# Post-normed products with tokens in the rows, and four tiles of the next products side by side

## The chip, the cores and the metric

The kernel runs on one core of a Trainium2 chip. The metric is the device time of one execution in microseconds. TensorE (PE) multiplies matrices into PSUM, which has eight banks of 512 fp32 columns; VectorE (DVE), ScalarE (ACT) and GpSimd (POOL) work on rows of 128 partitions; SyncE (SP) issues the loads. [...]

## What is computed

A block with a post-normed mixer and a post-normed feed-forward, followed by two layers of a second block, for 256 tokens of 1024 features. The change touches the first block and the start of the second:

```python
y = concatenate([out_a, out_b, out_c], axis=-1) @ w_out[l]
x = x + rmsnorm(y, norm_post_mix[l])
h = rmsnorm(x, norm_pre_ffn[l])
f = square(relu(h @ w_ff1[l])) @ w_ff2[l]
x = x + rmsnorm(f, norm_post_ffn[l])
# second block, layer 0, begins with
x = x + 0.5 * swiglu(rmsnorm_2(x, ffn_norm1[0]), ffn1_wg[0], ffn1_wu[0], ffn1_wd[0])
```

## The kernel before

The residual is kept as `x[k]`, eight tiles of 128 features by 256 tokens (features in the partitions). Every product is made of three matmuls on parts rounded to fp32r: `xh` (rounded) and `xl` (what is left) of the data, `wh` and `wl` of the weights: wh*xh, wh*xl, wl*xh (`mm_t`, lines 134 to 141; `mm_n`, 143 to 151, has the tokens as the stationary operand and 128 tokens in the rows of the result). A pre-norm is not applied to x: its gain goes into xh and xl, and its factor per token into the result.

Weights come through the class `Stream` (72 to 129) in one fixed order. `dma` loads a chunk of up to 2048 columns on SyncE into one of three buffers; `split` casts a part of 1024 columns on ScalarE (line 102); `low` subtracts on VectorE (line 112) and, after a chunk's last part, issues the next load; there are six slots (`HL`) for split parts. `get(ahead)` first splits until `ahead` more parts than the one asked for are there (4 by default), then returns the part. `low` of a part is written out when the next part is split, or in `get` when at most two parts are in hand. `fill` splits up to six parts with the subtraction on GpSimd.

The order of the instructions on each engine is the order in which the program writes them (`manual_schedule`, line 154), so a wait holds up all that is written later for the same engine. The tile pools add the semaphores; a new PSUM tile waits for a bank that is no longer read.

**The mixer's end** (791 to 818). The gating matmuls (line 796) make mixed tiles 0 to 2. `out_proj` (451) makes eight feature tiles of y, 24 matmuls of 256 columns each; `y_evac` (478) squares each in ScalarE and adds the squares up on GpSimd (`add_sq`, 193), and copies y times its gain. Then four blocks of 24 short matmuls for the position bias (`t5_mm`, 512) lie between the column sums (`colsum`, line 219), mean (226), power -0.5 on GpSimd (188), the diagonal matrix `dg` (234), and a matmul that broadcasts the factors to all rows (239). `post_add` (526) multiplies y by it, adds it to x on VectorE or GpSimd, and makes xh on ScalarE and xl on VectorE, tile by tile.

**The feed-forward** (828 to 894). The first two tiles of h @ w_ff1 are made side by side, k by k, as xh and xl arrive (841 to 845); then 15 pairs of tiles follow (852), each with its evacuation `ev_ff` (834), the squares of x for the pre-norm, and the bias blocks' evacuation `t5_evac` (521). The second product makes eight feature tiles of 96 matmuls each and ends like the mixer.

**`ffn2`** (383 to 434) is the second block's feed-forward. At its first call `start` (920) makes the squares of x; the gate and the up tile of the first pair are made one after the other for k = 0 to 6, then both for k = 7; then follow the second pair, with the column sums between its halves, the broadcast, two evacuations, and the loop over 20 more pairs.

## Time and profile before

| | |
|---|---|
| median of 3 runs | 1280.71 us (1280.48 to 1282.17) |
| profiled execution | 1278.97 us, its span 1277.1 us |
| TensorE, matmuls | busy 1250.2 us, 98% of the span |
| VectorE | busy 846.4 us, 66% |
| ScalarE | busy 661.3 us, 52% |
| GpSimd | busy 197.3 us, 15% |
| granted TensorE clock, mean | 0.989 of full |
| loads | 208.71 MB, 164 GB/s over the span |

Times are microseconds from the span's start. Busy time of TensorE includes the tail of each matmul, which overlaps the next, so the distance between two starts tells the rate. "PEld" is the load of the stationary operand. In a row of the waits, the engine and line ahead of the arrow stood idle until the one behind it was done. `L139` is line 139 of the kernel. A group by line and form gives the count, the busy time, the mean of one in ns, and the idle time ahead of them. [...]

### The profile page before, as it was taken

What the parts mean: (1) busy time and instruction counts of PE and PEld (TensorE: products, weight loads), DVE (VectorE), ACT (ScalarE), POOL (GpSimd) and SP (SyncE); (2) the same over time, 40 slices, a digit from 0 to 9 for tenths busy, and PEclk for the clock granted to TensorE, in tenths of its full rate; (3) what the DMA queues carried; (4) which work ended last, traced back from release to release, by engine and by line L of the source; (5) the groups of instructions that cost most, each with busy time, mean ns of one, the idle gap of its engine ahead of it and who ended that gap; (6) DMA issues with size and microseconds to landing.
All of it is one profiled execution on the core that took longest, in us unless ns stands there. A gap on an engine that the chain in (4) does not pass through costs nothing.

```text
span 1277.1 us, 24835 instructions
## 1 busy us (share of the span) xinstructions
PE 1250.2 (98%) x10316; PEld 1202.9 (94%) x10316; DVE 846.4 (66%) x1490; ACT 661.3 (52%) x1174; POOL 197.3 (15%) x192
## 2 busy tenths in 40 slices
PE   8999899999899999999999999999999989999998
PEld 7879899999799999977999999999999868999998
DVE  6886676654587666676766666666666796666553
ACT  5557465444345444565654444545454787554442
POOL 4424210110420001210300001100001462100000
PEclk9999899999899999999999999999999999999999
DMA  7534355555135545530455546556556411555463
GB/s 233 194 105 160 104 195 196 200 208 188 67 132 199 199 139 192 208 123 34 165 198 199 177 157 205 191 178 217 168 163 204 165 66 67 181 186 195 157 199 107
DMA packets 37265, 211.37 MB, mean 166 GB/s; under 512 B 4768, under 2 KB 8224, under 8 KB 18848
## 3 DMA queue, kind: packets, MB, share of 16 engines
q1 hardware_dynamic: 37152, 209.78, 48.3%
q8 instruction: 81, 1.33, 0.4%
q14 instruction: 32, 0.26, 0.1%
HBM read 208.71 MB, written 1.05 MB: 164 GB/s over the span
## 4 chain that ended last, share of the span: by engine, by line
PE 88%; DVE 6%; issue 2%; ACT 2%; DMA 1%; POOL 0%; SPq 0%; ACTq 0%; POOLq 0%; DVEq 0%
PE ps L139 26%; PE ps L140 26%; PE ps L141 26%; DVE wl L112 2%; PE ps L297 2%; PE ps L323 2%; PE ps L308 1%; PE ps L149 1%; PE ps L150 1%; PE ps L151 1%; PE ps L325 1%; ACT wh L102 1%; DVE dg L234 0%; PE ps L219 0%; DVE kc L1169 0%
## 5 line engine op out<-in xcount | busy, mean ns | idle before, releaser
L139 PE MATMUL ps<-xh,wh 128*128 128x256 f32 (+1 forms) x1848 | 523.0, 283 | 1.6 <-ACT xh L531 1.6
L140 PE MATMUL ps<-xl,wh 128*128 128x256 f32 (+1 forms) x1848 | 520.3, 282 | 1.5 <-DVE xl L538 0.8
L141 PE MATMUL ps<-xh,wl 128*128 128x256 f32 (+1 forms) x1848 | 518.9, 281 | 2.4 <-DVE wl L112 2.4
L112 DVE TENSOR_TENSOR wl<-raw,wh 128x1024 fp32r<-128x1024 f32 (+3 forms) x434 | 489.2, 1166 | 46.4 <-ACT wh L102 45.4
L102 ACT CAST wh<-raw 128x1024 fp32r<-128x1024 f32 (+4 forms) x436 | 400.2, 959 | 62.5 <-PE ps L140 26.5
L139 PEld LDWEIGHTS ps<-xh,wh 128*128 128x128 f32 (+1 forms) x1848 | 350.3, 190 | 5.3 <-issue 3.2
L140 PEld LDWEIGHTS ps<-xl,wh 128*128 128x128 f32 (+1 forms) x1848 | 349.8, 189 | 3.4 <-DVE xl L538 2.0
L141 PEld LDWEIGHTS ps<-xh,wl 128*128 128x128 f32 (+1 forms) x1848 | 350.0, 189 | 2.7 <-DVE wl L112 2.6
L139 PE MATMUL ps<-ah,wh 128*128 128x256 f32 x960 | 267.8, 279 | 0.0
L140 PE MATMUL ps<-al,wh 128*128 128x256 f32 x960 | 267.8, 279 | 0.0
L141 PE MATMUL ps<-ah,wl 128*128 128x256 f32 x960 | 267.8, 279 | 0.0
L139 PEld LDWEIGHTS ps<-ah,wh 128*128 128x128 f32 x960 | 180.4, 188 | 0.0
L140 PEld LDWEIGHTS ps<-al,wh 128*128 128x128 f32 x960 | 180.4, 188 | 0.0
L141 PEld LDWEIGHTS ps<-ah,wl 128*128 128x128 f32 x960 | 180.4, 188 | 0.0
L199 POOL TENSOR_TENSOR acc<-acc,sq 128x256 f32<-128x256 f32 x42 | 49.9, 1188 | 587.0 <-ACT sq L198 586.9
L393 ACT ACTIVATE s<-t 128x256 f32<-128x256 f32 x88 | 36.8, 418 | 191.9 <-DVE t L391 191.9
L391 DVE TENSOR_TENSOR t<-ps,rb 128x256 f32<-128x256 f32 x88 | 37.2, 423 | 73.5 <-PE ps L141 68.2
L213 DVE TENSOR_TENSOR al<-f,ah 128x256 fp32r<-128x256 f32 (+1 forms) x105 | 48.9, 466 | 52.8 <-ACT ah L212 52.8
L212 ACT CAST ah<-f 128x256 fp32r<-128x256 f32 (+1 forms) x105 | 45.9, 437 | 55.8 <-DVE f L395 43.2
L252 ACT ACTIVATE xh<-x,cols 128x256 fp32r<-128x256 f32 x40 | 20.4, 510 | 102.6 <-DVE x L428 95.6
L395 DVE TENSOR_TENSOR f<-ps,s 128x256 f32<-128x256 f32 x88 | 37.3, 424 | 47.4 <-ACT s L393 47.4
L427 DVE SCALAR_TENSOR_TENSOR t<-ps,rb 128x256 f32<-128x256 f32 x32 | 13.6, 425 | 76.2 <-PE ps L141 76.2
(285 smaller groups left out, 1321.4 us busy)
## 6 DMA issues: line engine op xcount, KB each, us to landing
raw<-in_gu SPq DMA_DIRECT2D x88, 1024.0 KB, 4.9
raw<-in_dn SPq DMA_DIRECT2D x64, 704.0 KB, 4.3
raw<-in_ff SPq DMA_DIRECT2D x32, 1024.0 KB, 5.0
raw<-in_w_out SPq DMA_DIRECT2D x4, 1024.0 KB, 4.9
raw<-in_aq SPq DMA_DIRECT2D x4, 1024.0 KB, 5.1
raw<-in_a_out SPq DMA_DIRECT2D x4, 1024.0 KB, 5.0
raw<-in_b_out SPq DMA_DIRECT2D x4, 1024.0 KB, 4.8
raw<-in_w1q SPq DMA_DIRECT2D x6, 512.0 KB, 4.0
```

The costliest lines, as they stand in the source:

```text
L102: act.copy(h[:, :n], t)
L112: eng.tensor_tensor(out=lo, in0=t, in1=h.bitcast(F32), op=ALU.subtract)
L139: pe.matmul(ps, lhsT=h[:, c:c + m], rhs=x[0][k], start=s0, stop=False)
L140: pe.matmul(ps, lhsT=h[:, c:c + m], rhs=x[1][k], start=False, stop=False)
L141: pe.matmul(ps, lhsT=lo[:, c:c + m], rhs=x[0][k], start=False, stop=s1)
L199: gp.tensor_tensor(out=acc, in0=acc, in1=sq, op=ALU.add)
L212: act.copy(h, src)
L213: dve.tensor_tensor(out=lo, in0=src, in1=h.bitcast(F32), op=ALU.subtract)
L297: pe.matmul(ps[:, o:o + n], lhsT=u["q"][:, i * P:i * P + P], rhs=u["k"][:, :n], start=True, stop=True)
L391: dve.tensor_tensor(out=t, in0=g, in1=rb, op=ALU.mult)
L393: act.activation(out=s, in_=t, func=AF.Silu)
L395: dve.tensor_tensor(out=f, in0=u, in1=s, op=ALU.mult)
```

## The change

- `w_out` and `w_ff2` are packed so that a part holds 512 columns of w for two rows-tiles (feed-forward), or 1024 columns for one (mixer). `mm_y` makes their products with 128 tokens of the data as the stationary operand and 512 features moving: four PSUM banks `py[tt][h]` hold y with tokens in the rows.
- In the mixer the k-tiles run in the order 3 to 7, 0 to 2; the gating matmuls stand behind the third of them; the last two run bank by bank.
- A Square with a running sum on ScalarE (`y_sq`) replaces the squares, their sums on GpSimd and the column sums. `y_rstd` makes the factors. `y_scale` copies y out of PSUM times the factor of its row, ScalarE for the first 128 tokens and VectorE for the others. There is no diagonal and no broadcast.
- `PostAdd.turn` transposes one feature tile of y with two TensorE transposes; VectorE multiplies by the gain and adds x; `prep` (250) makes xh, the square of x and its sum, and xl of the tile before.
- `PostAdd.products` makes four tiles of the next products side by side in two banks: two turns ahead of each k from 1 to 3, and one split at k = 4. Ahead of it stand the fourth bias block and four `get` calls, which leave five (4, 3, 2, 1 ahead) parts in hand.
- `ffn2` takes these as its first two pairs (`begun`), makes the third pair with the column sums between, and builds `dg` on ScalarE. The bias blocks are evacuated one pair later in the feed-forward, and in `ffn2` from its fourth pair on.
- `fill`, `post_add`, `y_evac`, `start` and the squares of x inside the loops are gone.

The diff, cut to its core:

```diff
-        def fill(self):
-            while self.ns < self.ng + HL and self.split(gp):
-                pass
...
+    def mm_y(banks, w, n, x, kts, first, last):
+        for tt in range(2):
+            for j in range(len(banks[tt])):
+                h, lo = w
+                ts = slice(tt * P, tt * P + P)
+                for i, k in enumerate(kts):
+                    c = (i * len(banks[tt]) + j) * n
...
+                    pe.matmul(ps, lhsT=x[0][k][:, ts], rhs=h[:, c:c + n], start=s0, stop=False)
+                    pe.matmul(ps, lhsT=x[1][k][:, ts], rhs=h[:, c:c + n], start=False, stop=False)
+                    pe.matmul(ps, lhsT=x[0][k][:, ts], rhs=lo[:, c:c + n], start=False, stop=s1)
...
+            if begun:
+                p = bank()
+                mm_t(p[:, :T], ws.get(), 0, P, X, range(KT), True, True)
+                _, rs = norm_cols(acc)
+                dg = tp.tile([P, T], F32, tag="dg", bufs=1, name="dg")
+                for tt in range(2):
+                    act.activation(out=dg[:, tt * P:tt * P + P], in_=ident, func=AF.Copy, scale=rs[:, tt:tt + 1])
+                mm_t(p[:, T:], ws.get(), 0, P, X, range(KT), True, True)
+                rb = bcast(rs, dg=dg)
+                for j, p in enumerate(begun + [p]):
+                    evac(j, p[:, :T], p[:, T:], rb)
...
+    def y_sq(ps, ss, tt, h, junk):
+        act.activation(out=junk, in_=ps, func=AF.Square, accum_out=ss[:, h, tt:tt + 1])
...
+        ms = sm.tile([P, 2], F32, tag="ms", bufs=3, name="ms")
+        dve.scalar_tensor_tensor(out=ms, in0=ss[:, 1], scalar=1.0 / D, in1=s0, op0=ALU.mult, op1=ALU.add)
+        rs = sm.tile([P, 2], F32, tag="rs", bufs=3, name="rs")
+        rstd_pow(rs, ms, 2)
...
+    def y_scale(ps, y, rs, pieces):
+        for h, o, n in pieces:
...
+            act.activation(out=dst[0], in_=src[0], func=AF.Copy, scale=rs[:, 0:1])
+            dve.tensor_scalar(out=dst[1], in0=src[1], scalar1=rs[:, 1:2], scalar2=None, op0=ALU.mult)
...
+        def turn(self):
...
+            ps = bank()
+            for tt in range(2):
+                pe.transpose(ps[:, tt * P:tt * P + P], self.y[tt][:, d * P:d * P + P], ident)
+            dve.scalar_tensor_tensor(out=x[d], in0=ps[:, :T], scalar=gcol(self.gi, d), in1=x[d], op0=ALU.mult, op1=ALU.add)
+            prep(d, self.gnext, self.acc)
+            if d == KT - 1:
+                prep_end()
+        def products(self, outs, w):
+            for k in range(KT):
+                if k:
+                    self.turn()
+                    self.turn()
+                for i, (p, wi) in enumerate(zip(outs, w)):
+                    mm_t(p, wi, 0, P, X, [k], k == 0 and i % 2 == 0, k == KT - 1 and i % 2 == 1)
+                if k == 4:
+                    ws.split()
+                    ws.low()
...
+        w = [ws.get(), ws.get(3)]
+        ws.low()
+        for tt in range(2):
+            for h in range(2):
+                for i in range(2):
+                    mm_y([[py[tt][h]] if t == tt else [] for t in range(2)], [v[:, 512 * h:512 * h + 512] for v in w[i]], 512,
+                         (oh, ol), [MIX_ORDER[KT - 2 + i]], False, i == 1)
+                y_sq(py[tt][h], ss, tt, h, pp.tile([P, 512], F32, tag="s", bufs=2, name="junk"))
+        t5 = [t5_mm([o5[:, i]]) for i in range(3)]
+        rs_y = y_rstd(ss, None)
+        y_scale(py, y, rs_y, ((0, 0, T), (0, T, T)))
+        acc = new_acc()
+        add = PostAdd(y, 1, 2, acc)
+        add.turn()
+        add.turn()
+        y_scale(py, y, rs_y, ((1, 0, 2 * T),))
         t5.append(t5_mm([o5[:, 3]]))
-        acc = post_add(ys, rb, 2)
+        w = [ws.get(HL - 2 - i) for i in range(4)]
+        p = [bank() for _ in range(2)]
+        add.products([b[:, o:o + T] for b in p for o in (0, T)], w)
```

The feed-forward's end has the same lines as the mixer's, behind `mm_y` over two halves of 16 parts, with `ws.get()` for each part and `ws.low()` after it in the second half.

## Rows read from the trace of the kernel before

**Rows 1.** TensorE's waits, whole run: who waited <- for whom: us, times, longest.
```profile
PE ps L239 <- DVE dg L234: 6.1, 3, 2.7
```

**Rows 2.** Windows at boundary 1: us, busy (count) by engine, granted clock, DMA share, GB/s.
```profile
131.00:139.50 8.50, 5.13 (x109) 4.45 (x107) 5.43 (x11) 3.64 (x6) 3.35 (x3) 0.95 0.43 153
139.50:145.50 6.00, 5.95 (x28) 5.95 (x29) 5.42 (x12) 3.05 (x6) 4.96 (x6) 0.51 0.01 3
```

**Rows 3.** Timeline at boundary 1: start, us, engine, operation, [idle before <- releaser].
```profile
130.99 0.87 PE L517 MATMUL ps<-rbd,o 128*128 128x64 bf16 x24
...
132.77 0.16 DVE L226 TENSOR_SCALAR ms<-ps 128x2 f32<-128x2 f32 x1 [1.38 <-PE ps L219]
...
133.00 0.71 POOL L188 TENSOR_TENSOR rs<-ms,mhalf 128x2 f32<-128x2 f32 x1 [3.21 <-DVE ms L226]
...
133.69 2.34 POOL L112 TENSOR_TENSOR wl<-raw,wh 128x1024 fp32r<-128x1024 f32 x1
...
133.75 2.56 DVE L234 TENSOR_SCALAR dg<-kon,rs 128x128 f32<-128x128 f32 x2 [0.82 <-POOL rs L188]
...
136.36 0.70 PE L239 MATMUL ps<-dg,kon 128*128 128x256 f32 x2 [2.21 <-DVE dg L234]
...
138.57 0.58 PE L139 MATMUL ps<-xh,wh 128*128 128x256 f32 x1 [0.81 <-ACT xh L531]
...
153.39 0.28 PE L139 MATMUL ps<-xh,wh 128*128 128x256 f32 x1
...
158.99 0.28 PE L139 MATMUL ps<-xh,wh 128*128 128x256 f32 x1
```

**Rows 4.** Windows at boundary 2, same columns as group 2.
```profile
321.80:329.50 7.70, 4.61 (x108) 4.18 (x106) 4.15 (x8) 2.80 (x5) 3.03 (x2) 1.00 0.14 55
329.50:336.50 7.00, 6.21 (x21) 4.98 (x22) 6.38 (x16) 4.09 (x9) 5.26 (x6) 0.52 0.00 0
336.50:340.00 3.50, 3.50 (x18) 3.50 (x18) 3.29 (x6) 2.25 (x8) 2.35 (x3) 0.50 0.02 5
```

**Rows 5.** Timeline of TensorE at boundary 2.
```profile
321.85 0.87 PE L517 MATMUL ps<-rbd,o 128*128 128x64 bf16 x24
...
349.23 0.70 PE L239 MATMUL ps<-dg,kon 128*128 128x256 f32 x2 [1.18 <-DVE dg L234]
...
355.37 0.28 PE L139 MATMUL ps<-xh,wh 128*128 128x256 f32 x1
```

**Rows 6.** Timeline of TensorE, products of 512 columns in latent attention; ten intervals.
```profile
1001.48 0.40 PE L150 MATMUL ps<-wh,cl 128*128 128x512 f32 x1
...
1003.80 0.40 PE L151 MATMUL ps<-wl,ch 128*128 128x512 f32 x1
```

**Rows 7.** Timeline of TensorE, four transposes in attention and what follows.
```profile
97.17 0.60 PE L308 MATMUL ps<-kon,p 128*128 128x128 f32 x4
...
97.70 0.65 PE L323 MATMUL ps<-pt,vm 128*64 128x256 f32 x2
```

**Rows 8.** Groups by line and form: count | busy us, mean ns | idle before.
```profile
L486 ACT ACTIVATE y<-ps,cols 128x256 f32<-128x256 f32 x16 | 7.7, 482 | 0.0
...
L836 ACT ACTIVATE t<-ps 128x512 f32<-128x512 f32 x15 | 9.0, 599 | 23.4 <-PE ps L141 23.4
...
L271 ACT ACTIVATION_READ_ACCUMULATOR p<-s,nm 128x1 f32 x44 | 8.3, 190 | 0.0
...
L427 DVE SCALAR_TENSOR_TENSOR t<-ps,rb 128x256 f32<-128x256 f32 x32 | 13.6, 425 | 76.2 <-PE ps L141 76.2
...
L252 ACT ACTIVATE xh<-x,cols 128x256 fp32r<-128x256 f32 x40 | 20.4, 510 | 102.6 <-DVE x L428 95.6 <-DVE x L470 6.8
...
L261 DVE SCALAR_TENSOR_TENSOR xl<-x,cols,xh 128x256 fp32r<-128x256 f32 x44 | 22.6, 514 | 15.4 <-ACT xh L252 14.2 <-ACT xh L531 1.2
...
L102 ACT CAST wh<-raw 128x1024 fp32r<-128x1024 f32 x293 | 295.7, 1047 | 30.4 <-PE ps L140 15.1 <-DMA raw<-in_w1q 6.4 <-DMA raw<-in_w1k 2.7
...
L112 DVE TENSOR_TENSOR wl<-raw,wh 128x1024 fp32r<-128x1024 f32 x291 | 360.9, 1273 | 39.0 <-ACT wh L102 38.5
```

More of the change, by code (lines that the diff above doesn't have):

```diff
@@ L380, in warm_table, with ffn2 @@
         act.activation(out=t, in_=mhalf[:, 0:1], func=func)
-    def ffn2(acc, gnext, extra=(), start=None, more=()):
+    def ffn2(acc, gnext, extra=(), begun=None):
         extra = list(extra)
@@ L597, in block_kernel @@
         mem = [mem_[:, k] for k in range(KT)]
-        mh = [mp.tile([P, T], F32R, tag=f"mh{k}", name=f"mh{k}") for k in range(KT)]
+        mh_ = mp.tile([P, KT, T], F32R, tag="mh", name="mh")
+        mh = [mh_[:, k] for k in range(KT)]
         ml_ = mp.tile([P, KT, T], F32R, tag="ml", name="ml")
@@ new lines, in block_kernel @@
+        while not pipe.done():
+            pipe.step()
+        y_ = mp.tile([P, 2, D], F32, tag="mh", name="y")
+        y = [y_[:, tt] for tt in range(2)]
+        ss = sm.tile([P, 2, 2], F32, tag="ss", name="ss")
+        py = [[bank() for _ in range(2)] for _ in range(2)]
+        for i, k in enumerate(MIX_ORDER):
+            if i == 3:
+                gmlp_out()
+                warm_table(AF.Silu)
+            if i < KT - 2:
+                mm_y(py, ws.get(), 512, (oh, ol), [k], i == 0, False)
@@ new lines, in block_kernel @@
+        w = [ws.get(), ws.get(3)]
+        ws.low()
+        for tt in range(2):
+            for h in range(2):
[4 more added lines that the diff above has]
+        t5 = [t5_mm([o5[:, i]]) for i in range(3)]
@@ L889, in block_kernel @@
-        dve.tensor_tensor(out=fy, in0=fy, in1=r2, op=ALU.mult)
-        dg = diag(fy)
-        ws.fill()
-        rb = bcast_ps(dg)[:, :T]
+        ss = sm.tile([P, 2, 2], F32, tag="ss", name="ss")
+        eps = sm.tile([P, 2], F32, tag="eps", name="eps")
+        dve.scalar_tensor_tensor(out=eps, in0=ms_f, scalar=EPS, in1=ms_f, op0=ALU.mult, op1=ALU.mult)
+        py = [[bank() for _ in range(2)] for _ in range(2)]
+        for h in range(2):
+            for i in range(16):
+                if h == 0 and i % 4 == 0:
+                    t5_mask(4 + i // 4, n5, o5[i // 4])
+                mm_y([[py[tt][h]] for tt in range(2)], ws.get(), 512, (AH, AL), [2 * i, 2 * i + 1], i == 0, i == 15)
+            if h:
+                ws.low()
+            for tt in range(2):
+                y_sq(py[tt][h], ss, tt, h, ft.tile([P, 2 * T], F32, tag="tf"[tt], name="junk"))
@@ L893, in block_kernel @@
+        t5 = [t5_mm(o5[i]) for i in range(3)]
+        rs_y = y_rstd(ss, eps)
+        y_scale(py, y, rs_y, ((0, 0, T), (0, T, T)))
+        acc = new_acc()
+        add = PostAdd(y, 3, g2("ffn_norm1_2", 0), acc)
+        add.turn()
+        add.turn()
+        y_scale(py, y, rs_y, ((1, 0, 2 * T),))
         t5.append(t5_mm(o5[3]))
-        acc = post_add(ys, rb, g2("ffn_norm1_2", 0))
+        w = [ws.get(HL - 2 - i) for i in range(4)]
+        p = [bank() for _ in range(2)]
+        add.products([b[:, o:o + T] for b in p for o in (0, T)], w)
@@ L916, in t5_step @@
                 return f
[L918 to L930 removed]
+            acc = ffn2(acc, g2("mix_norm_2", 0), [t5_step(j) for j in range(4, 16)], p)
         if upto == 3:
```

180 lines of the change are left out of this document (63 added, 117 removed), and 2 rows, old and new, of the table seq.

## The prediction

> **What bounds the kernel now.** TensorE is busy for 98% of the span, so a gain can come only from its pauses, its clock, or fewer cycles. The list of TensorE's waits is short, and its longest entry is the broadcast that waits for the diagonal `dg` [rows 1]. That sends the reader to the two places where a post-normed product meets the residual: the end of the mixer's output product (boundary 1, from 131 us) and the end of the first feed-forward (boundary 2, from 322 us). The windows show more there than the waits do: at boundary 1, 28 products take 6.0 us at a granted clock of 0.51 [rows 2]; at boundary 2, 21 products take 7.0 us and 18 more 3.5 us, all at about half clock [rows 4]. At full clock a product of 256 columns follows the one before it after 0.1167 us: 48 of them lie between 153.39 and 158.99 [rows 3]. I count from S, the end of the stream of products before each boundary (130.99 [rows 3], 321.85 [rows 5]), to the start of the 145th product behind it, so that both kernels have done the same work.
>
> Before, boundary 1: 158.99 - 130.99 = 28.0 us [rows 3]; 144 products alone are 16.8. The chain is to be seen in the same rows: the last Square, the sums, the power at 133.00, then the two diagonals, which take 2.56 us because GpSimd's split (2.34 us) runs beside them; the first product comes at 138.57, 7.6 us after S. Boundary 2: 355.37 - 321.85 = 33.5 us [rows 5]. It is dearer because one gate tile first consumes xh and xl as they arrive, three products at a time, and because a second broadcast waits 1.2 us [rows 5].
>
> **The change, part by part.** *Wider products.* 192 products of 256 columns become 96 of 512 in the mixer, 768 become 384 in the feed-forward. At full clock ten intervals of 512 columns take 2.32 us [rows 6], 0.232 each against 2 x 0.1167 = 0.2334: 480 x 0.0014 = 0.6 us saved (bounds 0 and 1.0). *Moved gating matmuls, moved sums of squares, changed weight order, later bias evacuations*: 0, since the stages where they lie are unbroken products, which cover them (the list of waits has nothing long there [rows 1]); without that cover an evacuation more, under 1 us. The residual's squares now sit in the chain and are counted there on ScalarE and GpSimd. Removed: 8+8 accumulations, the column sums at S, both diagonals and broadcasts, and GpSimd's splits.
>
> *The new chain*, the same at both boundaries. Square with a running sum over 512 columns: no row shows it; the Relu of 512 from PSUM is 0.60 and the read of a sum 0.19 [rows 8], so I take 0.86 between 0.6 and 1.1. From S: the last product's tail is 0.40 - 0.23 [rows 6], so Square starts at 0.2 and ends at 1.1; mean 0.16, power 0.71 [rows 3], 2.05; scaled copies of 256 columns on ScalarE, like those that made y, 0.48 [rows 8], 2.55. Meanwhile three of the four blocks of 24 bucket matmuls (0.87 each with its tail, 0.72 apart [rows 3]) cover TensorE until 2.2. Two transposes: four take 0.53 to the next instruction [rows 7], so 0.27 a pair and 0.42 to its end: 3.0. x: 0.43; xh: 0.51; xl: 0.51 [rows 8]. First product at 4.1, second (it needs xl0, queued behind x1 on VectorE) at 4.65. So 7.6 becomes 4.1.
>
> *The wait it adds.* Calling for the next weights puts splits between turn 1 and turn 2. At boundary 1 two of six slots are still to be split: ScalarE does xh, Square, xh, Square, the 512-column copy, then casts of 1.05 each [rows 8], done at 6.6 and 7.6. The fourth tile's products need the first of them: TensorE finishes nine products at 5.6 and stands until 6.65, then for the remainder (VectorE, 1.2; mean 1.27 [rows 8]) until 7.9. The second remainder, which nothing needs yet, ends at 9.05, and x2 and then xl1 are queued behind it: xl1 at 9.85. TensorE's second product of k=1 starts at 9.9; from there 83 products (9.7) and eight transposes (1.07) run without a gap, as VectorE needs 0.9 a turn against 1.9 of TensorE's work per two turns: 96 products at 20.65. Then 48 more (5.6) and 0.3 for weights whose split queues behind two evacuations (bounds 0 and 2.5): **26.55** against 28.0.
>
> At boundary 2 four parts were split in the loop, so one cast and one remainder lie there: 7.8, xl1 8.67, 96 products at 19.5. Then 48 (5.6), column sums, broadcast, and a wait for a PSUM bank (four bias banks, two of products, one of the third tile and the broadcast's make eight): 1.4, bounded by 0.4 and by 0.4 + 1.2 + 0.9 with the wait of [rows 5] and a block of [rows 3]: **26.5** against 33.5. The moved weight loads go out on SyncE when a remainder ends; their parts are needed after the 96 products, over 10 us later: 0.
>
> *The clock.* It fell before at about 138.6, after waits of 2.21 and 0.81 us with little more than a broadcast and one bucket block between them [rows 3]. The new kernel has such a stretch too: from 5.6 to 9.9 at boundary 1 four products and four transposes (1.0 us of 4.3), from 5.9 to 8.7 at boundary 2 one product and four transposes (0.65 of 2.8). [...] Boundary 1: 26.55 + 2.7 - 28.0 = +1.25. Boundary 2: 26.5 + 1.75 - 33.5 = -5.25.
>
> Sum: -0.6 + 1.25 - 5.25 = -4.6 us. The profiled run before took 1278.97 us (span 1277.1 and 1.9 around it), so 1274.4 for one like it; the median of the runs, 1280.71, stands 1.74 above it, so **1276.1**.
>
> **Rivals.** *A: the clock stays up* at boundary 2 (-6.4) or at both (-9.1): 1274.4 or 1271.6. For it: the stall there is 2.2 us, between full stretches. Against: it is as long as the longer of the two waits ahead of 138.6. *B: the transposes do not count as work for the clock (the slower side).* Place: the turns 4 to 7, two transposes between each dozen products of k=1 to 3. Rows: at boundary 2 the clock stayed low for the 21 products that came with waits between them, and rose only behind an unbroken run [rows 4]. If transposes break a run as waits did, the clock is low until k=4 and then for the same 28 or 18 products. Price: 35 products and eight transposes at half clock, 35 x 0.213 + 2.1 = 9.6 instead of 5.15, so 4.45 more at each boundary: -4.6 + 8.9 = +4.3 us, 1285.0. It decides from the point at which the low stretch outlasts turn 7 at both; at one alone the sum is about 0. For it: turns stand exactly where the clock must recover. Against: the transposes of attention come at full clock [rows 7], but few at a time and with many products between. [...] *C: weights late.* If the splits that queue behind the evacuations cost 1.2 to 2.5 at each boundary instead of 0.3, or GpSimd's sums slow VectorE as the split did [rows 3], 2 to 3 us of the gain are lost: 1278.5. *D: the change doesn't shorten the chain*, because the sum of squares waits for more than its own row (the Square's sum read late, bank of turn 0 reused by turn 1): at most 1 us a boundary, 1278.
>
> **How the numbers follow.** Forecast as summed 42%, A 23%, C and D 17%, B 18%. A measurement of this kernel tells about 0.2% (2.6 us) from no change, so faster means below 1278.1 and slower above 1283.3. The forecast (its own range 1274 to 1278) and A are faster, C and D lie at the edge, half each; B is slower in four parts of five. Faster 0.70, same 0.16, slower 0.14. The range takes in most of A and C and reaches to B: 1271.5 to 1284.
>
> **What would show it.** In the changed profile: the first product about 4 us after the stream's end at both boundaries; TensorE waiting for the fourth tile's cast and remainder and then for xl1 at boundary 1, for xl1 alone at boundary 2, with VectorE's remainder the last thing done ahead of x2; 145th product 29 and 28 us after S; two stretches at half clock of some 5 us or less; no VectorE operation of 2.5 us there; 512-column products 0.232 apart. The prediction is wrong if the clock never falls there, if it stays low past turn 7, if 512-column products come faster than 0.23, or if the splits are done by then.

## The result

The changed kernel takes 1266.03 us (median of 4 runs, 1264.1 to 1268.56) against 1280.6 us for the kernel before beside it: ratio 0.9900, 95% interval 0.9886 to 0.9915. The forecast was 1276.1 us, with a range from 1271.5 to 1284; the direction was right, the gain was about three times the 4.6 us forecast, and the time lies below the range. The profiled execution of the changed kernel has a span of 1264.1 us, 13.0 less than the 1277.1 before.

Where the 13.0 us lie can be read from the starts of TensorE's instructions in the two timelines. S is, as in the prediction, the end of the stream of products ahead of a boundary; the 145th product behind it marks equal work. The third column is an experiment told below (the changed kernel with its operands put back to their old place); each column adds up to the start of the last product.

| stretch, us | before | after | after, old place |
|---|---|---|---|
| start to S of boundary 1 | 130.99 | 131.57 | 130.35 |
| boundary 1: S to the 145th product | 28.00 | 28.03 | 27.59 |
| from there to S of boundary 2 | 162.86 | 163.31 | 163.29 |
| boundary 2: S to the 145th product | 33.52 | 26.45 | 28.00 |
| from there to the first down product | 111.66 | 110.55 | 110.53 |
| from there to the last product | 806.00 | 800.10 | 805.64 |
| sum | 1273.03 | 1260.01 | 1265.40 |

Two rows carry the gain. Boundary 2 gives 7.1 us. The last row gives 5.9, in a part of the kernel in which the change edits nothing of weight: there each of the four down stages (528 products with ah and al, the end of each feed-forward of the second block) takes 59.7 us where it took 61.5, 7.0 us together, and the other stages there give about 1 back.

TensorE's waits in the changed kernel, from the list of the whole run (engine, tile and line waited for: us in total, times, longest). The entry of [rows 1], the broadcast that waits for a diagonal, is gone; in its place stand the low part of x, a weight's low part and a weight's cast (of the second row only 0.8 us lie at a boundary, at 139.37 below; 1.6 us lie at 40.6 us, where the kernel before waits 2.4):

```profile
PE ps L136 <- DVE xl L271: 2.8, 3, 1.9
PE ps L137 <- DVE wl L113: 2.5, 3, 1.6
...
PE ps L135 <- ACT wh L103: 0.8, 1, 0.8
...
PE ps L135 <- ACT rb L255: 0.5, 1, 0.5
```

The windows that answer to [rows 2] and [rows 4] (us, busy and count by engine in the order PE, PEld, DVE, ACT, POOL, granted clock, DMA share, GB/s), of the changed kernel:

```profile
131.50:138.60 7.10, 5.92 (x113) 4.85 (x111) 3.56 (x8) 5.09 (x11) 1.44 (x2) 1.00 0.25 104
138.60:145.50 6.90, 5.82 (x26) 5.50 (x26) 4.45 (x9) 2.46 (x7) 1.51 (x2) 0.52 0.44 153
322.90:330.50 7.60, 6.28 (x118) 5.46 (x117) 4.17 (x8) 4.55 (x10) 1.45 (x2) 1.00 0.11 44
330.50:337.50 7.00, 6.04 (x52) 6.05 (x52) 5.62 (x14) 5.05 (x13) 4.08 (x5) 1.00 0.00 0
337.50:341.00 3.50, 3.50 (x33) 3.50 (x31) 1.50 (x2) 0.71 (x1) 0.81 (x1) 1.00 0.29 37
```

At boundary 1 the clock still falls to half (0.52 in the second row). At boundary 2, where it lay at 0.52 and 0.50 for 10.5 us before [rows 4], it stays at 1.00.

The timeline of boundary 1, changed kernel, S at 131.57 (start, us, engine, operation, idle before and releaser), answers to [rows 3]:

```profile
131.57 2.27 PE L583 MATMUL ps<-rbd,o 128*128 128x64 bf16 x72
131.83 0.60 ACT L501 ACTIVATE junk<-ps 128x512 f32<-128x512 f32 x1 [0.71 <-PE ps L161]
132.32 0.19 ACT L501 ACTIVATION_READ_ACCUMULATOR junk<-ps 128x1 f32 x1
...
132.79 0.69 POOL L198 TENSOR_TENSOR rs<-ms,mhalf 128x2 f32<-128x2 f32 x1 [10.40 <-DVE ms L511]
...
135.60 0.39 PE L135 MATMUL ps<-xh,wh 128*128 128x256 f32 x1
...
137.03 1.98 ACT L103 CAST wh<-raw 128x1024 fp32r<-128x1024 f32 x2
138.09 2.36 DVE L113 TENSOR_TENSOR wl<-raw,wh 128x1024 fp32r<-128x1024 f32 x2 [1.37 <-ACT wh L103]
...
138.12 0.39 PE L135 MATMUL ps<-xh,wh 128*128 128x256 f32 x1 [0.79 <-ACT wh L103]
...
139.37 0.58 PE L137 MATMUL ps<-xh,wl 128*128 128x256 f32 x1 [0.76 <-DVE wl L113]
...
140.42 0.48 DVE L538 SCALAR_TENSOR_TENSOR x<-ps,cols,x 128x256 f32<-128x256 f32 x1
...
140.82 0.48 DVE L271 SCALAR_TENSOR_TENSOR xl<-x,cols,xh 128x256 fp32r<-128x256 f32 x1
...
141.35 0.58 PE L136 MATMUL ps<-xl,wh 128*128 128x256 f32 x1 [0.33 <-DVE xl L271]
...
145.73 0.28 PE L137 MATMUL ps<-xh,wl 128*128 128x256 f32 x1
...
146.56 0.60 PE L537 MATMUL ps<-kon,y 128*128 128x128 f32 x4
```

The chain is short: power at +1.2 us from S, first product at +4.0. Then the two splits stand between turn 1 and turn 2, as read from the code: TensorE waits for the fourth weight's cast (138.12) and low part (139.37), and VectorE comes to x2 (140.42) and then xl1 (140.82) only behind both low parts, so that the second product of k=1 starts at 141.35. A product lasts 0.28 again from 145.73, which is before turns 6 and 7 (the four transposes at 146.56).

### The profile page after: what moved, and what is told of

It reads as the page before. It is cut to its first block, busy times and chain, and to the rows that moved or that the text cites. A ratio compares the mean times of both kernels' runs of the same rounds, so it can differ in the third digit from the quotient of the medians.

```text
span 1264.1 us, 23830 instructions
## 1 busy us (share of the span) xinstructions
PE 1242.1 (98%) x9844; PEld 1172.2 (93%) x9844; DVE 837.7 (66%) x1482; ACT 658.2 (52%) x1164; POOL 174.7 (14%) x169
## 4 chain that ended last, share of the span: by engine, by line
PE 85%; DVE 9%; ACT 3%; issue 2%; DMA 1%; POOL 0%; SPq 0%; ACTq 0%; DVEq 0%
PE ps L135 23%; PE ps L136 22%; PE ps L137 22%; DVE wl L113 3%; PE ps L159 3%; PE ps L161 3%; PE ps L160 3%; PE ps L307 2%; PE ps L333 2%; PE ps L318 1%; ACT wh L103 1%; DMA raw<-in_w1q 1%; PE ps L145 1%; PE ps L147 1%; PE ps L146 1%
## 5 line engine op out<-in xcount | busy, mean ns | idle before, releaser
L113 DVE TENSOR_TENSOR wl<-raw,wh 128x1024 fp32r<-128x1024 f32 (+4 forms) x436 | 489.8, 1162 | 60.7 <-ACT wh L103 60.2
L137 PE MATMUL ps<-ah,wl 128*128 128x256 f32 x704 | 194.6, 276 | 0.0
L136 PE MATMUL ps<-al,wh 128*128 128x256 f32 x704 | 194.6, 276 | 0.0
L135 PE MATMUL ps<-ah,wh 128*128 128x256 f32 x704 | 194.6, 276 | 0.0
L137 PEld LDWEIGHTS ps<-ah,wl 128*128 128x128 f32 x704 | 132.2, 188 | 0.0
L135 PEld LDWEIGHTS ps<-ah,wh 128*128 128x128 f32 x704 | 132.2, 188 | 0.0
L136 PEld LDWEIGHTS ps<-al,wh 128*128 128x128 f32 x704 | 132.2, 188 | 0.0
L209 POOL TENSOR_TENSOR acc<-acc,sq 128x256 f32<-128x256 f32 x49 | 55.2, 1126 | 527.4 <-ACT sq L208 526.8
L262 ACT ACTIVATE xh<-x,cols 128x256 fp32r<-128x256 f32 x56 | 28.5, 510 | 107.9 <-DVE x L449 90.8
```

The costliest lines, as they stand in the source:

```text
L113: eng.tensor_tensor(out=lo, in0=t, in1=h.bitcast(F32), op=ALU.subtract)
L135: pe.matmul(ps, lhsT=h[:, c:c + m], rhs=x[0][k], start=s0, stop=False)
L136: pe.matmul(ps, lhsT=h[:, c:c + m], rhs=x[1][k], start=False, stop=False)
L137: pe.matmul(ps, lhsT=lo[:, c:c + m], rhs=x[0][k], start=False, stop=s1)
L209: gp.tensor_tensor(out=acc, in0=acc, in1=sq, op=ALU.add)
```

## The experiments

**The place of the operands.** The down stages' code is the same in both kernels. What differs is where their moving operands lie: the change needs one slot of 32 bytes more in the pool `sm`, and every tile allocated behind that pool, `ah`, `al`, `oh` and `ol` among them, stands 32 bytes further on in the built program. Four runs move tiles and nothing else. In the kernel before and in the changed one (32 bytes; with `[P, 24]` 96 bytes):

```diff
     mhalf = lead.tile([P, 24], F32, name="mhalf")
+    sm.tile([P, 8], F32, name="pad")
```

and, for xh and xl in the changed kernel:

```diff
+    res.tile([P, 8], F32, name="pad0")
     xh = [res.tile([P, T], F32R, name=f"xh{k}") for k in range(KT)]
     xl = [res.tile([P, T], F32R, name=f"xl{k}") for k in range(KT)]
+    res.tile([P, 24], F32, name="pad1")
```

> The kernel before, with one unused tile of 32 bytes in the pool of small tiles: every tile that is allocated behind that pool (the operands ah/al of the down products, oh/ol of the output projections, the scratch of each stage) lies 32 bytes further on, as in the changed kernel; x, xh, xl, the weights and all instructions stay as they are. Theory (the place of the moving operand in SBUF sets the distance of the 256-column products): the four down stages of 528 products go from 61.5 to 59.7 us each (0.1167 to 0.1133 us a product), together -7.0 us, and the second ffn product, whose 768 products have ah and al as moving operands too, from 89.5 to 87.0 us; in sum about -9.6 us, 1271 us. Rival (the down products got faster by something else in the change, such as the other phase of the weight buffers after the second ffn product was cut into twice as many loads): all stages as before, 1280.6 us within 0.2%.

> The changed kernel with an unused 96 bytes in the pool of small tiles, which puts ah/al and oh/ol back on a multiple of 128 bytes, as they lay before the change, and moves nothing else. Theory of the operand's place: the four down stages go back to 61.5 us each, +7.0 us, about 1273 us; both boundaries as in the changed kernel. Rival (something else in the change): down stages stay at 59.7 us, 1266 us.

> The changed kernel with an unused 32 bytes in the pool of small tiles: ah/al and oh/ol lie 64 bytes behind a multiple of 128. Theory of the operand's place in its first form (any place off the multiple of 128 is fast): 59.7 us for each down stage, 1266 us. Its second form (64 bytes is as slow as 0): 61.5 us for each, 1273 us. Rival (something else in the change): 1266 us.

> The changed kernel with 32 unused bytes ahead of xh and xl and 96 behind them: xh and xl lie 32 bytes behind a multiple of 128 where they lay on one; ah/al and oh/ol stay 32 bytes behind a multiple. Theory of the operand's place: the products that have xh and xl as moving operands, about 5,500 of them, go from 0.1167 to 0.1133 us: each gate and up stage of 1056 products from 124.0 to about 120.4 us, the first ffn product by -2.6 us, in sum about -18 us where the weights' splits on VectorE and ScalarE keep up: 1248 us. Rival (the place has nothing to do with it): 1266 us.

The kernel before with 32 bytes: 0.9954 (0.9933 to 0.9976) of its own time, 1272.1 us, and all four down stages at 59.73 us. So the 7 us of the down stages come without the change; the rival falls. But its ten runs spread from 1266.9 to 1278.9 us, and its second ffn product got slower, 90.3 us for 89.5, not 87.0. The changed kernel with 96 bytes: 0.9981 (0.9969 to 0.9993), down stages 62.5 us; with 32 bytes: 1.0036 (1.0024 to 1.0048), slower than the kernel before, down stages 63.2. So the gain goes with the place, but a multiple of 128 is not what decides. And with xh and xl moved, 0.9960 (0.9945 to 0.9975), my theory failed: the products with xh and xl did not get faster but slower (0.1178 us for 0.1167), and three of the four down stages took 62.1 us with their operands at the same place as in the first, which took 59.7. Something besides the place of the moving operand had to be at work.

Three kernels of products alone measure it by itself; their inner part is

```python
for k in range(KT):
    m, w = slice(mo + k * T, mo + k * T + T), slice(wo + k * P, wo + k * P + P)
    pe.matmul(ps, lhsT=wh[:, w], rhs=mh[:, m], start=k == 0, stop=False)
    pe.matmul(ps, lhsT=wh[:, w], rhs=ml[:, m], start=False, stop=False)
    pe.matmul(ps, lhsT=wl[:, w], rhs=mh[:, m], start=False, stop=k == KT - 1)
```

> A kernel of nothing but products, which leaves out the whole reference: groups of 24 float32r products of 256 columns (the three of each k as in the kernel: high by high, high by low, low by high) run in stretches of 192 behind a product of 64 columns. Between stretches only the place of the operands changes: the stationary ones lie 96, 0, 32 and 64 bytes behind a multiple of 128, and for each of these the moving ones 0, 32, 64 and 96. The 16 stretches run three times: with all other engines idle, with loads, casts and differences at the rate of the down stage beside them, and idle again. Theory (the operands' place sets the pace): the pace goes with the place, the same in all three rounds; with the stationary operands at 96, moving ones at 0 take 0.1167 us a product, at 32 0.1133, at 64 0.120. Rival 1 (other engines' traffic sets it): one pace in the two idle rounds wherever the operands lie, and slower ones in the middle round. Rival 2 (the pace is a rhythm that a stretch falls into by chance, whatever the place): paces between 0.1133 and 0.120 that differ between the rounds for the same places.

The paces (the time from one product's start to the next) were 0.1167 to 0.1209 us by place, and each of the 16 pairs of places gave the same in all three rounds to 0.0004 us. The loads wait for nothing of TensorE's and ran in the first round instead of the second; the windows of the first and the third round (columns as above) show that traffic and no traffic make no difference:

```profile
30.00:370.00 340.00, 340.00 (x2875) 340.00 (x2874) 136.20 (x116) 114.20 (x115) 0.00 (x0) 1.00 0.46 173
...
750.00:1100.00 350.00, 350.00 (x2958) 350.00 (x2957) 0.00 (x0) 0.00 (x0) 0.00 (x0) 1.00 0.00 1
```

That is 0.1183 us a product in the first and 0.1183 in the third. So the other engines' traffic is out as a cause for these products. The figures for the three places were missed (0.1189, 0.1209 and 0.1184 us for 0, 32 and 64). Here the low parts lay 128 bytes, modulo 256, behind the high ones; the next two runs avoid that, and no run shows what it does by itself.

> A kernel of nothing but products, which leaves out the whole reference: stretches of 72 float32r products of 256 columns, the stationary operands at 0, 32, ... 224 bytes and the moving ones at 0, 32, ... 224 bytes behind a multiple of 1024, all 64 pairs, each behind a product of 64 columns and again behind one of 128. Theory (the place alone sets the pace): the two paces of a pair agree to 0.0005 us; paces go from 0.1133 to 0.121 us. Rival (rhythms): many pairs have two paces.

> A kernel of nothing but products, which leaves out the whole reference: stretches of 96 float32r products of 256 columns, the stationary operands at the place modulo 1024 bytes that the weights have in the kernel (224), the moving ones at 0, 32, 64, 96, 128 or 160. Ahead of each stretch stands one product of 64, 16, 32, 128 or 200 columns, or a pause in which TensorE waits for a copy on ScalarE; then stretches of different places follow one another without any break. Theory (the place alone sets the pace): one pace for each place, whatever stands ahead of it; 0.1133 us at 32 and 160, 0.1167 at 0, 0.120 at 64. Rival (a place allows several rhythms; which one a stretch falls into goes by what ran ahead of it, and it stays until something breaks it): two or more paces at the same place, such as 0.1133 and 0.1178 at 32, by the product or the pause ahead; without a break, the pace of a place goes by the place before it.

All 64 pairs of places, twice. What counts is not either place but their distance, moving minus stationary, modulo 256 bytes. Two pairs of starts, 48 products apart, with the stationary operand at 96 bytes in both: the moving one at 96 (distance 0), then at 32 (distance 192):

```profile
258.43 0.28 PE L87 MATMUL ps<-mh,wh 128*128 128x256 f32 x1
...
264.19 0.28 PE L87 MATMUL ps<-mh,wh 128*128 128x256 f32 x1
```

```profile
241.46 0.28 PE L87 MATMUL ps<-mh,wh 128*128 128x256 f32 x1
...
246.90 0.28 PE L87 MATMUL ps<-mh,wh 128*128 128x256 f32 x1
```

5.76 us and 5.44 us, 0.1200 and 0.1133 us a product. Each distance has 16 stretches; their paces (starts of products, worked out from the timeline):

```
distance   pace, us a product (number of stretches of 16)
   0       0.1200 (16)
  32       0.1167 (10), 0.1178 (6)
  64       0.1178 (15), 0.1133 (1)
  96       0.1200 (16)
 128       0.1187 (13), 0.1200 (3)
 160       0.1187 (8), 0.1173 (7), 0.1200 (1)
 192       0.1133 (14), 0.1178 (2)
 224       0.1183 (16)
```

49 of the 64 pairs had one pace, 15 had two: neither theory has it alone. The distance sets which paces there are, and some distances have two. In the other kernel the choice differs with what ran before: in one row of stretches without a break, moving operands at distance 32, 64, 32, 64 give 0.1167, 0.1133, 0.1167, 0.1133; after four more stretches, at 192, 32, 96 and 32, the same distance 64 gives 0.1178. In two more such rows, behind a product of another width and behind a pause, it has 0.1178 from the start. Distance 192, which comes behind 64 in each of the three rows, has 0.1178 there every time. Two times 48 products at distance 64 in the first row, the second time behind those stretches:

```profile
870.11 0.28 PE L89 MATMUL ps<-mh,wl 128*128 128x256 f32 x1
...
875.55 0.28 PE L89 MATMUL ps<-mh,wl 128*128 128x256 f32 x1
...
948.52 0.28 PE L89 MATMUL ps<-mh,wl 128*128 128x256 f32 x1
...
954.17 0.28 PE L89 MATMUL ps<-mh,wl 128*128 128x256 f32 x1
```

5.44 us and 5.65 us. The rows of the instructions look alike; only their starts tell the two apart. A pause ahead of a stretch also changes the choice: at distance 192 five products of different widths ahead all gave 0.1133, the pause 0.1178, both times. What stands right ahead doesn't settle it alone: at distance 32 the product of 64 columns gave 0.1178 in the first of the two rounds and 0.1167 in the second.

In the kernels the weights lie at 224 modulo 256. This puts the runs into one scheme (paces of the down stages; the last two rows are edits told below, whose operands lie as in the changed kernel):

| kernel | ah, al at | distance | pace of the down stages |
|---|---|---|---|
| before | 0 | 32 | 0.1167 |
| before + 32 bytes | 32 | 64 | 0.1133 |
| after | 32 | 64 | 0.1133 |
| after + 32 bytes | 64 | 96 | 0.1200 |
| after + 96 bytes | 128 | 160 | 0.1187 |
| after, xh and xl moved | 160 | 192 | 0.1133 in the first, 0.1178 in three |
| after, low part early | 32 | 64 | 0.1178 in the first, 0.1133 in three |
| after, turns first | 32 | 64 | 0.1178 in the second, 0.1133 in three |

With xh and xl moved these stand at distance 64 and run at 0.1178; three of the down stages behind them keep that pace, but the first, behind products at 0.1178 too, does not. In the last two rows the one slow down stage is the one whose gate and up products end at 0.1178, where they end at 0.1167 ahead of the fast ones. So distance 64 can fall either way, and that the changed kernel had 0.1133 there in all four down stages was not sure beforehand; what makes the choice is not shown. That the ten runs of the kernel before with 32 bytes differ by 12 us because some stages fell into 0.1178 fits (a stage of 528 products then takes 62.1 us for 59.7, so four are 9.4 us), but only one of the ten has a trace, so it is argued, not shown.

If distance 192 holds 0.1133 in most stretches (14 of 16 in the table), all 256-column products should be put there (in the kernel before the first line alone is needed):

```diff
+    res.tile([P, 40], F32, name="pad0")
     xh = [res.tile([P, T], F32R, name=f"xh{k}") for k in range(KT)]
     xl = [res.tile([P, T], F32R, name=f"xl{k}") for k in range(KT)]
+    res.tile([P, 56], F32, name="pad1")
```

> The kernel before with 160 unused bytes ahead of xh and xl, which brings all moving operands of the 256-column products to 192 bytes, modulo 256, behind the stationary ones; nothing of the change is in it. Theory (place, not the change): every 256-column product at 0.1133 us instead of 0.1167, down stages 59.7 us, gate and up stages 120.4 us, first and second ffn product 90 and 87 us; some 8,900 products by 0.0034 us are -30 us, less what the start and the attention stages don't give back: 1253 us. Rival (the other rhythm, 0.1178 us): +8 us, 1289 us.

The kernel before at distance 192: 0.9835 (0.9819 to 0.9852), 1257.2 us, 21 us less without touching an instruction, and more than the whole change gave. The gate and up stages behind the first take 120.6 to 121.5 us for 124.0 to 124.9, the down stages 59.7. It is less than the 30 us summed since the second ffn product fell into 0.1178 (90.3 us) and the attention stages gave little.

**What the change alone is worth.** Two runs take the place out of the comparison: the changed kernel at its old place (224 bytes in `sm`), and the changed kernel at distance 192 like the kernel before just told.

> The changed kernel with 224 unused bytes in the pool of small tiles: ah, al, oh and ol lie at the same place modulo 256 as in the kernel before, so that what is left between the two is the change's instructions alone. Theory (the change itself gives what its two boundaries show, +0.5 us at the first and -8.2 us at the second): down stages at 61.5 us, about 1273 us, -7 to -8 us against before. Rival (the sum that was forecast, with the clock falling at the second boundary, holds once the place is taken out): 1276 us, -4 to -5 us.

> The changed kernel with all moving operands of the 256-column products 192 bytes, modulo 256, behind the stationary ones, as in the two runs before it, one with the early weights and one of the kernel before. Theory (the change and the place add up): gate and up stages 120.4 us, down stages 59.7 us; against the kernel before at the same place (1257.2 us) the change gives -7 to -9 us: 1248 to 1250 us; the early splits were worth another 9 us (1238.7 us). Rival (the stalls at the boundaries drop TensorE into the slower rhythm, and the early splits prevent it): some stages at 0.1178 us a product, 1255 us or more.

At the old place: 0.9941 (0.9925 to 0.9957), 1271.8 us against 1280.06; by the ratio that is 7.5 us with an interval from 5.5 to 9.6 (the medians differ by 8.3). The down stages are back at 61.5 us. At distance 192 the changed kernel has 0.9770 (0.9726 to 0.9813), 1248.7 us, 8.4 us below the 1257.2 of the kernel before at the same distance; its four runs go from 1246.0 to 1253.7, so this is the looser of the two. Both say the same: the change is worth 7 to 8 us, as both expectations had it. The parts of the first came out otherwise: +0.5 us at boundary 1 and -8.2 at boundary 2 were expected; at the old place it is 0.0 from the first S to the second and -6.65 from there to the first down product. Two starts of the same line, 48 products apart, in a down stage of the kernel before, of the changed kernel, and of the changed kernel at the old place:

```profile
480.33 0.28 PE L139 MATMUL ps<-ah,wh 128*128 128x256 f32 x1
...
485.93 0.28 PE L139 MATMUL ps<-ah,wh 128*128 128x256 f32 x1
```

```profile
480.31 0.28 PE L135 MATMUL ps<-ah,wh 128*128 128x256 f32 x1
...
485.75 0.28 PE L135 MATMUL ps<-ah,wh 128*128 128x256 f32 x1
```

```profile
480.06 0.28 PE L135 MATMUL ps<-ah,wh 128*128 128x256 f32 x1
...
485.66 0.28 PE L135 MATMUL ps<-ah,wh 128*128 128x256 f32 x1
```

5.60, 5.44 and 5.60 us: 0.1167, 0.1133, 0.1167 each.

In the profile at the old place the clock did fall at boundary 2, though the code and the wait there are the same as in the changed kernel's profile. Its windows behind S (321.23):

```profile
321.20:329.00 7.80, 6.31 (x118) 5.46 (x117) 4.35 (x9) 4.56 (x10) 1.45 (x2) 1.00 0.13 54
329.00:336.00 7.00, 6.22 (x40) 6.22 (x41) 4.17 (x11) 3.68 (x10) 3.00 (x4) 0.76 0.00 0
```

With the 0.50 of [rows 4] as the low level, 0.76 over 7 us is 3.4 us of it, an estimate. The 97th product comes 20.80 us after S there and 19.25 in the changed kernel's profile: the fall costs 1.55 us.

**The stalls that the change leaves.** Both boundaries still wait for splits and for xl1. Two edits, first the low part alone (behind both pairs of turns), then the splits too:

```diff
         add.turn()
         add.turn()
+        prep_end()
```

```diff
-        w = [ws.get(), ws.get(3)]
+        w = [ws.get(5), ws.get(4)]
...
-        w = [ws.get(HL - 2 - i) for i in range(4)]
+        w = [ws.get(HL - 3 - i) for i in range(4)]
...
                 if k == 4:
                     ws.split()
+                    ws.split()
                     ws.low()
```

> The changed kernel with only the first of the two edits: the low part of x1 is issued right behind the second turn at both boundaries; the splits stay where they are. Theory (at the second boundary TensorE waits for that low part, which stands behind a weight's difference and x2 on VectorE; at the first it waits for the fourth weight's cast and difference as well): at the second boundary -1.5 to -2 us, at the first less than 1 us, since the wait for the fourth weight stays. Rival (the low part is all that matters at both): -3 us or more at the first boundary.

> The changed kernel with two edits at both boundaries: the low part of x1 is issued right behind the second turn (it waited for x2), and no weight is split between the turns: at the first boundary one split more is made ahead of the last mixer products, and the second split of each boundary comes at k = 4. Theory (the stalls at k = 0 and k = 1, which end on the splits and on that low part, are all that is left at the boundaries): at the first boundary the third to fifth waits go, the 12 products of k = 1 no longer run at half clock, -3 to -4 us; at the second the wait of 1.9 us goes, -1.5 to -2 us; 1261 us. Rival (the turns' chain on VectorE and ScalarE, 0.95 us for each k, is next in line): TensorE waits for x2 and x3 instead, and less than 1.5 us is gained in both, 1265 us.

With the low part alone, in one run (1261.81 us), the 145th product comes 24.84 us after S at boundary 1 (28.03 in the changed kernel) and 25.25 at boundary 2 (26.45); with the splits moved too, 22.69 and 24.26. The whole kernel then takes 1257.5 us, ratio 0.9834 (0.9815 to 0.9854) to the kernel before; the theory held in kind, and its figures were too small (3 to 4 and 1.5 to 2 us expected, 5.3 and 2.2 measured). At boundary 1 the rival of the first expectation came out: the low part alone gives 3.2 us (2.75 to 3.7 against the four profiles that have this boundary unchanged, with xh and xl at the same place), although the wait for the fourth weight stays (cast 0.8, low part 0.8 us). At boundary 2 it gives 1.2, less than the theory had. The windows show why it is more than the wait (first two rows: low part alone, boundary 1; second two: both edits, boundary 1):

```profile
129.80:137.00 7.20, 5.90 (x112) 4.85 (x111) 4.19 (x9) 5.23 (x11) 1.43 (x2) 1.00 0.24 97
137.00:144.00 7.00, 6.36 (x54) 6.36 (x55) 6.69 (x14) 4.84 (x13) 3.42 (x5) 1.00 0.42 152
```

```profile
131.00:138.00 7.00, 6.61 (x123) 5.92 (x122) 4.09 (x10) 3.66 (x10) 1.44 (x2) 1.00 0.69 257
138.00:145.00 7.00, 7.00 (x62) 7.00 (x62) 5.86 (x12) 6.36 (x14) 4.92 (x6) 1.00 0.00 1
```

The clock, 0.52 for 6.9 us in the changed kernel, stays at 1.00 in both. It fell at boundary 1 in all six profiles of kernels that leave this boundary as the change has it, and in none of the three with the low part early. So the second product of k=1 comes 1.2 us earlier (8.60 for 9.78 behind S), and the other 2.0 of the 3.2 us are, by difference, the fall that doesn't come. With both edits TensorE has no wait over 0.2 us left between 125 and 160 us.

**The order of the turns.**

```diff
             for k in range(KT):
-                if k:
-                    self.turn()
-                    self.turn()
+                self.turn()
+            for k in range(KT):
                 for i, (p, wi) in enumerate(zip(outs, w)):
```

> The changed kernel with all eight turns ahead of the first product at both boundaries, so that the four products side by side no longer run between the turns; nothing else changes. Theory (the gain at the second boundary comes from hiding the turns' chain beside the products, and from the clock that stays up with it): the first product comes 3.5 to 5 us later at each boundary, and the granted clock falls at the second as it did before the change, for some 7 us; in sum +4 to +6 us at each boundary. Rival (the products' order is free, since the turns' last part would hide under the first products anyway): the first product comes later but the 97th by less than 1.5 us at each boundary, and the clock stays up at the second.

In its one run (1274.15 us) the first product comes 6.9 us later at boundary 1 (10.92 after S for 4.03) and 5.8 at boundary 2; the 145th only 2.2 and 3.25. That lies between both expectations: two thirds of the delay are made up at boundary 1 and somewhat under half at boundary 2, where the clock fell too, since the products behind the turns hardly wait. The turns themselves do, since the splits stand between turn 1 and turn 2 here too; the largest entry of its waits at these lines:

```profile
PE ps L537 <- DVE x L538: 5.4, 3, 3.1
```

The clock at boundary 2 fell in that run (0.76 in the second row; S at 324.76):

```profile
324.70:333.00 8.30, 5.04 (x110) 4.21 (x110) 4.81 (x10) 4.66 (x11) 1.44 (x2) 1.00 0.11 44
333.00:340.00 7.00, 6.30 (x38) 5.83 (x39) 6.42 (x13) 5.70 (x13) 4.77 (x6) 0.76 0.01 2
```

Since it fell in the changed kernel at the old place too, this run doesn't show that the products side by side keep the clock up.

**All together.** Early weights and distance 192:

> The kernel with the splits moved and the low part of x1 issued early, and with unused bytes ahead of and behind xh and xl, so that all moving operands of the 256-column products (xh, xl, ah, al, oh, ol) lie 192 bytes, modulo 256, behind the stationary ones; ah, al, oh and ol lay 64 behind them, xh and xl 32. Theory (the distance between the two operands modulo 256 sets the pace, and at 192 it is 0.1133 us in nearly all stretches of products alone): each gate and up stage of 1056 products goes from 124.0 to 120.4 us, the first ffn product from 0.1167 to 0.1133 us a product (-2.4), the down stages stay at 59.7 us, the second ffn product (there the weights move) goes from 89.4 to 87.7 us as in the run with xh moved by 32; in sum -18 us or somewhat more, 1239 us. Rival (the kernel's stalls leave TensorE in the other rhythm of that distance, 0.1178 us): gate and up stages 125 us, down stages 62 us, +12 us, 1269 us.

1238.65 us (1238.62 to 1239.85), ratio 0.9691 (0.9676 to 0.9705): 39.5 us below the kernel before by that ratio, 27 below the changed one, and within 0.4 us of what was expected. Two starts 48 products apart in a gate and up stage, where [rows 3] has 5.60 us:

```profile
649.84 0.28 PE L135 MATMUL ps<-xh,wh 128*128 128x256 f32 x1
...
655.28 0.28 PE L135 MATMUL ps<-xh,wh 128*128 128x256 f32 x1
```

5.44 us. The gate and up stages behind the first take 120.5 to 121.4 us, all down stages 59.7, the second ffn product 87.7.

## Why the forecast missed

The error is 10.1 us (1276.1 against 1266.0). The run at the old place splits it: the forecast's own subject, the change at an unchanged place, came to -7.5 us (-5.5 to -9.6) against the -4.6 of the sum; the rest is the pace of the down stages.

**The pace of untouched products: the step that failed.** The prediction took "0.1167 us" as a property of a 256-column product at full clock [rows 3] and put every stage that the diff doesn't edit at 0. That product's pace goes with where its two operands lie (0.1167 us at distance 32, 0.1133 in the down stages of the changed kernel at 64), and an added small tile moved one of them: -7.0 us in the profiled run. No rival held this. All long stretches of the trace before run at distance 32 and at 0.1167. It holds only a faint sign of a second pace, a few dozen products at 0.1178, such as the 24 between these two starts, at full clock:

```profile
340.05 0.28 PE L140 MATMUL ps<-xl,wh 128*128 128x256 f32 x1
...
342.87 0.28 PE L140 MATMUL ps<-xl,wh 128*128 128x256 f32 x1
```

What could have been done is to compare the addresses of the two programs.

In the kernels of products alone the pace was 0.1133 to 0.1200 us by the distance between the two operands, at equal work and with all other engines idle. What inside the chip makes it so isn't shown.

**The new chain: right.** Forecast from S: first product 4.1, second 4.65, fourth weight's cast 6.65, its low part 7.9, second product of k=1 9.9 at boundary 1 and 8.67 at boundary 2. Measured: 4.03, 4.55, 6.55, 7.80, 9.78 and (from 322.91) 8.54. The Square that no row showed took 0.60, and 0.68 up to the end of its sum's read (0.19, which overlaps it), for the 0.86 that were taken. The splits, in number and order, were read from the code as they ran.

**Boundary 2: right but for the clock.** Forecast 26.5 us with the clock up, 28.25 with the fall. Measured 26.45 in the changed kernel's profile, where it stayed up (the first part of rival A, which had 1.75 us less), and 28.00 at the old place, where it fell. The price of the fall, 1.75, taken from the 18 products of [rows 4] at up to 0.214 us for 0.117, was 1.55 in these two profiles. Whether it falls there isn't fixed by the code of the boundary: of six kernels with this same boundary and this same wait, one profile each, it fell in two (97th product 20.8 to 20.9 us after S), and stayed up in four (19.0 to 19.3).

**Boundary 1: the term for the clock was too large.** Forecast 26.55 + 2.7 = 29.25, measured 28.03, and 27.59 at the old place. The 2.7 us are a fall as long as the one before the change, 28 products at 0.214 us for 0.117 [rows 2]; no run of the new chain shows one of that length. The 97th product came at 22.43 and 21.99 instead of 20.65 + 2.7 = 23.35: the fall cost 1.8 and 1.3 us, since 18 products started at half clock in the changed kernel's profile and 11 at the old place, not the 28 of [rows 2]. The other 0.3 are the late splits after the 96 products, which did not stall: 5.60 us for the 48.

**Rival B: refuted.** It had the clock low until turn 7 was past. At boundary 1 it rose at about 145.6, between two pairs of turns (143.86 and 146.56), with turns in the middle of the stretch from which it rose, and at boundary 2 it did not fall in the changed kernel's run. At the old place, where it fell there, it was back by the second product behind turns 6 and 7, with no stay at half clock beyond them:

```profile
334.51 0.68 PE L538 MATMUL ps<-kon,y 128*128 128x128 f32 x4
...
335.15 0.28 PE L136 MATMUL ps<-xl,wh 128*128 128x256 f32 x1
```

Four transposes at a time between a dozen products did not hold the clock down here: at boundary 1 of the changed kernel it was 0.50 from 143.8 to 145.4 us, with one pair of turns in it, 0.88 from there to 146.5, and 1.00 from 146.5 to 148.5, with the next pair in it. A run of transposes alone isn't among these.

**Wider products: no saving.** Put at -0.6 (480 x 0.0014 is 0.67). The second ffn product took 89.36 us for 89.48, 0.2333 for each of its 383 intervals and so just two of 256 columns; the mixer's output stage took 25.4 for 25.0, with the gating matmuls now inside it. The row that priced them [rows 6], 0.232, is of other operands, and this pace goes by place as well: 87.67 us, 0.2289, in the run with xh and xl moved, where ah and al lay elsewhere too.

**Moved bias evacuations: -0.7 where 0 stood.** The prediction found nothing long in the list of waits where these lie. The kernel before has two waits for the bias masks there, 1.7 us behind boundary 2:

```profile
PE ps L517 <- DVE o L510: 1.7, 2, 0.9
```

They became one of 0.3 (111.66 to 110.55 us), and the stretch between the boundaries got 0.45 us longer. Of -7.6 us between the profiles at the old place, boundary 1 gives 0.4, boundary 2 5.5, these 0.7; the last 1.0 lie ahead of boundary 1 and behind the first down product, and no run here tells their cause.

**Two slips beside the sum.** By the shares as given faster comes to 0.735 and same to 0.12, not 0.70 and 0.16; and rival B's place has two transposes between one dozen products and the next, where two turns, four transposes, stand (its price does count them). Neither moves the forecast.

## What to carry to other kernels

Ahead of costing any change, compare the addresses of the tiles that the longest streams read, in both built programs: a small tile that is added or dropped moves everything allocated behind it, and with it, as here, the pace of code that the change doesn't touch (32 bytes: 61.5 to 59.7 us for a down stage). Measure the pace of the streams at a few distances between moving and stationary operand, choose the best on purpose (here 192 bytes modulo 256 for 256 float32r columns, 21 us of 1280), look in the trace whether the pace came (0.1178 occurs at 192 too), and compare kernels at one and the same distance. In a boundary, list what stands between two turns on each queue: here an early low part, one line, brought the second product of k=1 at boundary 1 1.2 us forward and gave 3.2 us in all, and the granted clock stayed at 1.00 there.

## What the hardware showed

- In unbroken streams of float32r products of 256 columns the pace goes with the distance between the two operands, modulo 256 bytes: 0.1133 to 0.1200 us in the run of all 64 pairs of places, at a mean granted clock of 0.998, 6% between the best and the worst. Loads, casts and differences beside the products changed nothing (0.1183 us with and without, at a granted clock of 1.00).
- Some distances had two paces in these runs (0.1133 and 0.1178 at 64 and 192, 0.1167 and 0.1178 at 32). Which one a stretch took differed with what ran ahead of it (at distance 192 in one run 0.1133 behind a product, 0.1178 behind a pause), by a rule that these runs don't show, and it lasted for whole stages: 59.7 us in the changed kernel and 62.1 in the run with the low part early for the first down stage, 528 products with the same operands at the same addresses.
- The same wait of 2.3 us at boundary 2 (k=0's end to the second product of k=1, a few products and transposes in it) was there in six kernels, and the clock fell in two of them (0.76 over 7.0 us at the old place) and not in four (1.00 in the changed kernel). At boundary 1 it fell in all six (0.52 over 6.9 us in the changed kernel, 0.76 over 7.0 at the old place), and in none of the three kernels whose low part of x1 comes early (1.00).
